# Feature tiles that stream both parts of the tokens behind one weight load

## The chip, the cores and the metric

One core of a Trainium2 chip runs the whole program. The metric is device time in microseconds, the median of a few runs on the chip. Beside the runs there is one profiled execution, with the start and length of every instruction.

## The reference

The reference computes two transformer blocks over 256 tokens of 1024 features, all in float32. The matrix products that matter here are projections of normed tokens `h`:

```
f  = (silu(h @ w_g) * (h @ w_u)) @ w_down            # twice, d_ff = 2816
q, k, v, z, xs, b, c, dt = split(h @ w_in)           # stick-breaking attention and a state-space mixer
xbc = silu(conv4(concat(xs, b, c)) + conv_b)         # depthwise, causal, 4 taps
q = h @ xa_wq ; k, v = split(mem_n @ xa_wkv)         # cross attention on a memory of 256 rows
c_gate, hc, b_gate, q, f_pre, v, g = split(h @ w_in_2)
u = c_gate * hc ; y = b_gate * conv3(u)              # and a gated recurrence that takes sigmoid(f_pre)
q = (h @ wq) ; scores = q . keys ; top 16 pairs      # 16384 experts: gelu(h . u_e) * gate, times v_e
```

Between the stages stand root-mean-square norms and residual sums. The answer must keep float32 accuracy.

## The kernel before

**Precision.** TensorE multiplies operands of a rounded float32 type. So the kernel splits each operand into a rounded part (hi) and what is left (lo), and forms hi x hi, hi x lo and lo x hi. The tokens' two parts are `uT[0]` and `uT[1]`, features on partitions: 8 tiles of 128 features by 256 tokens each. A weight *unit* is 128 x 1024 numbers, loaded by a DMA into `raw`, and split by `prefetch` (L127): ScalarE writes hi (L142), VectorE the rest lo (L143). A ring of slots holds split units some tiles ahead of their use.

**Kinds of product.** `half_chunk` and `acc_step` take tokens as the stationary operand and 512 columns of a unit as the moving one. A *feature tile* (`f_tile`, L297) is the other way round: 128 columns of the weight are stationary, and 256 tokens move through. It runs over 8 feature tiles k and makes three matmuls in each, all into the first half of one PSUM bank: w_hi x u_hi, w_hi x u_lo, w_lo x u_hi. Every matmul has its own weight load. Two banks `mm` alternate, so a tile needs the bank that the second-last tile left. After the 24 matmuls the function `evac` that the caller gave takes the result out of PSUM: one instruction on ScalarE or VectorE that also scales, adds a bias, or applies Silu, Sigmoid or a product.

**Where feature tiles stand.** In order of time: 36 in the first feed-forward stage (`features`, L499, a gate and an up tile by turns), 16 `qk` (L830), 1 `dt` (L836), 8 `xs` and 4 `bc` (L857, each with a 4-tap convolution in `conv`, L844), 8 `mk` (L906, from the memory's `memT`), 8 `xq` (L996), 36 in the second feed-forward stage, 4 `f2` (L1182, Sigmoid), 4 `q2` (L1187), 12 `chb` (L1202 to L1206, triples that end in a 3-tap convolution, L1191), 12 `pq` (L1433), and 128 `pu`, the experts' first table (L1477).

**What sets the order.** The program is written out by hand: each engine runs its instructions strictly in the order in which the Python code makes them. `tick` is called in the middle and at the end of a tile; after a given amount of products it takes the next step of each *side* (a generator with work of another kind, such as `attention`, `steps`, `hgrn`, `short_conv`), and at the end of a tile also the next split. So in the queue of VectorE and of ScalarE the order is: what the middle of the tile added, `evac` of the tile, the sides' steps at its end, the split.

**Side work that matters here.** `attention` (L570) walks through L585 (products), L596 and L597 (exponential, logarithm), L599 and L600 (sums on VectorE), L602 and L603 (split), L607 (products of the running sums), L611, L620. `steps` works on `dt`; L653 to L661 are its copies on VectorE. `hgrn` begins with a table load (L1035), four products on VectorE (L1038) and a logarithm (L1040), then L1042 and four scans (L1044). `short_conv` begins with transposes of the convolved tile (L1147), which PE meets in its own order.

Of the kernel before, what the change touches and what calls it, by code (L numbers as in the profile page):

```python
# [100 lines left out]
class Builder:  # L101
# [25 lines left out]
    def prefetch(self, n=1):  # L127
        """The parts of the next n units: rounded, and what is left."""
# [38 lines left out]
    def extend(self, slots, raws):  # L167
        """More places for units, split and just loaded, in the free parts of the arenas."""
        self.retired = False
        self.live = len(self.slots) + slots  # L170
        for _ in range(slots):
            b = self.RA.alloc(2048)
            self.free.append(len(self.slots))
            self.extra[len(self.slots)] = b
            self.slots.append((b.ap[:, 0:1024], b.ap[:, 1024:2048]))
        for _ in range(raws):
            b = self.FA.alloc_top(1024)
            self.raw_free.append(len(self.raw))
# [19 lines left out]
    def tick(self, us, split=True):  # L198
        """After us of products were issued: the next split, and as much of the side work."""
# [22 lines left out]
    def add_side(self, gen, rate):  # L222
        """gen yields where other work may come between, after 1 / rate us of it or what it yields."""
# [13 lines left out]
    def settle(self):  # L237
        """All but the norms at the end of a stage."""
# [20 lines left out]
    def half_chunk(self, u0, t, aT, evac, hook=None):  # L259
        """512 columns: [tokens, 512] for token tile t, from four units."""  # L260
# [29 lines left out]
    def opening(self, u0, aT, evacs, before_t1):  # L290
        """Two chunks, the first token tile of both ahead of the second."""
# [4 lines left out]

    def f_tile(self, u, aT, evac):  # L297
        """128 columns: [columns, 256 tokens], from one unit."""
# [35 lines left out]
    def acc_gemm(self, u0, pairs, n, done=None, mid=None, tail=6, early=1, before_t1=None, have=None):  # L334
        """[tokens, 1024] += one unit for each (features tile, index in it, position) of pairs. have(k): the
        features that unit k takes are there, for the first token tile."""
# [38 lines left out]
    def transposes(self, src, t, dst, col=None, kt0=0, n=8, part=None):  # L375
        """Tokens of tile t by features -> features by tokens, in two parts, times the gain."""
# [28 lines left out]
    def halves_rstd(self, ss):  # L405
        """From the two halves of a mean of squares."""
# [11 lines left out]
    def resid(self, t, row, ss):  # L418
        """h += rmsnorm(acc) * row; the mean squares of the new h to ss."""
# [21 lines left out]
    def normed(self, t, ss, hn):  # L441
        """h of token tile t, divided by its root mean square."""
# [20 lines left out]
    def ffn(self, name, row_name, before_t1, done, mid):  # L463
        """h += rmsnorm(swiglu(rmsnorm(h))) / 2."""
# [34 lines left out]
        def features(c):  # L499
            act[c] = self.tpair(2)  # L500
            ac = abs_[c % 2].v(j=2, t=256)
            for j in range(2):
                u, sg = u0 + FFN_AT["gu", c] + 2 * j, sgs[j].ap
                self.f_tile(u, uT, lambda ps: nc.scalar.activation(sg, ps, AF.Silu))
                self.f_tile(u + 1, uT, lambda ps: nc.vector.tensor_mul(ac[:, j], ps, sg))
# [63 lines left out]
    def attention(self, par, qT, kT, vt, oat, ready):  # L569
        """Stick-breaking attention, two heads at a time, keys on partitions."""  # L570
# [58 lines left out]
    def steps(self, dtb, dtT):  # L629
        """dt and its running sums, tokens on partitions."""  # L630
# [23 lines left out]
        # the sums with heads on partitions, in three parts that add up  # L654
# [23 lines left out]
    def ssd(self, xp, zt, oT, ready):  # L678
        """xp: [channels, 12, 3+256] convolved; y for both chunks, gated, normed, transposed."""
# [20 lines left out]
        # states after the first chunk  # L700
# [109 lines left out]
    def mixer(self, before_t1, done, mid):  # L810
# [10 lines left out]
        mblocks, memT = self.tpair(8)  # L821
# [7 lines left out]
        for f in range(8):  # L829
            self.f_tile(FIRST["qk"] + 2 * f, uT,  # L830
                        lambda ps: nc.scalar.activation(qT[:, f], ps, AF.Copy, scale=0.125))
            self.f_tile(FIRST["qk"] + 2 * f + 1, uT, lambda ps: nc.scalar.activation(kT[:, f], ps, AF.Copy))
# [3 lines left out]
        self.f_tile(FIRST["dt"], uT, lambda ps: nc.scalar.activation(  # L836
            dtT, ps[0:16], AF.Identity, bias=self.cols[0:16, COL["dt_bias"]:COL["dt_bias"] + 1]))
# [6 lines left out]
        def conv(f, ps):  # L844
            nc.scalar.activation(xp[:, f, 3:259], ps, AF.Copy)
# [10 lines left out]
        for f in range(8):  # L856
            self.f_tile(FIRST["xs"] + f, uT, lambda ps: conv(f, ps))  # L857
        for f in range(4):
            self.f_tile(FIRST["bc"] + f, uT, lambda ps: conv(8 + f, ps))
# [45 lines left out]
        for f in range(8):  # L905
            self.f_tile(FIRST["mk"] + f, memT, lambda ps: nc.vector.tensor_copy(kmT[:, f], ps))  # L906
# [18 lines left out]
    def cross(self, before_t1, kv, done, mid):  # L925
# [69 lines left out]
        for f in range(8):  # L995
            self.f_tile(FIRST["xq"] + f, uT,  # L996
                        lambda ps: nc.scalar.activation(qT[:, f], ps, AF.Copy, scale=0.0625))
# [31 lines left out]
    def hgrn(self, qh, ff, vt, gt, mix, ready):  # L1029
# [16 lines left out]
        # decays  # L1046
# [17 lines left out]
        # tokens by keys for the updates of the state  # L1064
# [17 lines left out]
        # states  # L1082
# [59 lines left out]
    def short_conv(self, f, y, yt, mix):  # L1142
        """The 128 channels of tile f: norm of their two groups, and to the features of mix."""
# [25 lines left out]
    def second(self, before_t1, done, mid):  # L1169
# [11 lines left out]
        for f in range(4):  # L1181
            self.f_tile(FIRST["f2"] + f, uT, lambda ps: nc.scalar.activation(ff[:, f], ps, AF.Sigmoid))  # L1182
# [3 lines left out]
        for f in range(4):  # L1186
            self.f_tile(FIRST["q2"] + f, uT, lambda ps: nc.scalar.activation(qh[:, f], ps, AF.Copy))  # L1187
# [3 lines left out]
        def conv(f, ps):  # L1191
            up, b = ups[:, f % 2], bg[:, f % 2]
            nc.scalar.activation(b, ps, AF.Copy)
# [6 lines left out]
        for f in range(4):  # L1200
            up = ups[:, f % 2]
            self.f_tile(FIRST["chb"] + 3 * f, uT,  # L1202
                        lambda ps: nc.scalar.activation(up[:, 2:258], ps, AF.Copy))
            self.f_tile(FIRST["chb"] + 3 * f + 1, uT,
                        lambda ps: nc.vector.tensor_mul(up[:, 2:258], up[:, 2:258], ps))
            self.f_tile(FIRST["chb"] + 3 * f + 2, uT, lambda ps: conv(f, ps))  # L1206
# [14 lines left out]
    def top16(self, lists):  # L1221
        """Of each list (source, its length, values, indices, scratch): the 16 best, in order."""
# [28 lines left out]
    def pick_head(self, sc, h):  # L1251
        """The 16 best pairs of keys of a head, both token tiles. Ranks (a, b) with more than 16 pairs at or
        above them are left out: for a = 0 all b stay, for a < 8 those under 8, and then b = 0."""
# [27 lines left out]
    def routing(self, kT):  # L1281
        """Experts and gates of both token tiles."""
# [3 lines left out]
        # places in the list of pairs -> ranks  # L1286
# [47 lines left out]
    def gates(self, kT, X):  # L1334
        """Gates of four tokens at a time, spread over all experts."""
# [34 lines left out]
    def peer(self):  # L1370
# [58 lines left out]
        for c in range(1, 4):  # L1429
            if c > 1:  # L1430
                self.finish(chunks[c - 2])
            for f in range(4):
                self.f_tile(FIRST["pq"] + 4 * c + f, hT, lambda ps: nc.scalar.activation(  # L1433
                    qT[c % 2][:, :, f], ps.rearrange("p (t n) -> p t n", t=2), AF.Copy))
# [324 lines left out]
```

## Time and profile before

| | |
|---|---|
| median of 3 runs | 1671.27 us (1669.7 to 1671.59) |
| span of the profiled execution, its own time | 1669.3 us |
| TensorE busy | 1652.0 us (99%) |
| VectorE busy | 1152.8 us (69%) |
| ScalarE busy | 981.0 us (59%) |
| GpSimd busy | 272.2 us (16%) |

The span runs from the first to the last instruction of the execution that the profiler recorded; no other time of that execution is given. A matmul's end is modelled and overlaps the next one's start, so the distance between starts tells more of TensorE's pace than its busy share. The granted TensorE clock is at its full level in all 40 slices of the page.

### The profile page before, as it was taken

To read this page: it belongs to the slowest core of one execution; us is meant where nothing else is said; L and a number is where in the kernel's file an instruction comes from. 1 tells how busy PE (TensorE), PEld (TensorE's weight loads), DVE (VectorE), ACT (ScalarE), POOL (GpSimd) and SP (SyncE) were. 2 spreads that over 40 slices of the span, in tenths; PEclk is the share of its full clock that TensorE was granted. 3 is DMA by queue.
4 is the path that set the end of the run, shared out by engine and by line. 5 is a ranking of instruction groups with operands and counts; after the bars stand their busy time and mean duration, and the time that the engine had idled before them with its cause. 6 is when DMAs were issued, how large, how long until landed. Compare 5 with 4: busy or idle time off the path is not lost.

```text
span 1669.3 us, 29176 instructions
## 1 busy us (share of the span) xinstructions
PE 1652.0 (99%) x11110; PEld 1504.8 (90%) x11110; DVE 1152.8 (69%) x2369; ACT 981.0 (59%) x1826; POOL 272.2 (16%) x312
## 2 busy tenths in 40 slices
PE   8999999999999999999999999999999999999998
PEld 6999899988898899989989999999999888888886
DVE  7555565876756755567657998899999855555554
ACT  7444476786555644457355564888877645545544
POOL 0000000000000000000100002988888100000000
PEclk9999999999999999999999999999999999999999
DMA  9565443354535856536234555445444555555553
GB/s 333 196 199 184 159 133 125 112 197 147 176 101 170 272 183 199 186 102 201 77 128 154 180 183 190 153 165 165 160 158 154 192 198 189 194 197 190 194 196 127
DMA packets 79325, 288.77 MB, mean 173 GB/s; under 512 B 8784, under 2 KB 8912, under 8 KB 79056
## 3 DMA queue, kind: packets, MB, share of 16 engines
q1 hardware_dynamic: 77904, 281.66, 50.9%
q10 hardware_dynamic: 1280, 5.24, 0.9%
q8 instruction: 87, 1.43, 0.4%
q14 instruction: 54, 0.44, 0.1%
HBM read 285.82 MB, written 1.05 MB: 172 GB/s over the span
## 4 chain that ended last, share of the span: by engine, by line
PE 93%; DVE 2%; ACT 2%; DMA 1%; issue 1%; POOL 0%; SPq 0%; POOLq 0%; ACTq 0%; DVEq 0%
PE mm L305 15%; PE mm L306 15%; PE mm L307 15%; PE acc L322 11%; PE acc L324 11%; PE acc L326 11%; PE mm L276 2%; PE mm L272 2%; PE mm L273 2%; PE sd L1356 2%; DMA raw<-ws 1%; DVE lo L143 1%; PE sd L383 1%; PE acc L585 1%; PE sd L1411 0%
## 5 line engine op out<-in xcount | busy, mean ns | idle before, releaser
L143 DVE TENSOR_TENSOR lo<-raw,hi 128x1024 fp32r<-128x1024 f32 x419 | 513.3, 1228 | 266.0 <-ACT hi L142 263.9
L305 PE MATMUL mm<-uT,hi 128*128 128x256 f32 x2024 | 580.9, 287 | 1.9 <-DVE X L1459 1.0
L306 PE MATMUL mm<-uT,hi 128*128 128x256 f32 x2024 | 571.2, 282 | 0.0
L307 PE MATMUL mm<-uT,lo 128*128 128x256 f32 x2024 | 571.1, 282 | 0.0
L142 ACT ACTIVATE hi<-raw 128x1024 fp32r<-128x1024 f32 x419 | 442.1, 1058 | 218.7 <-PE acc L326 185.6
L305 PEld LDWEIGHTS mm<-uT,hi 128*128 128x128 f32 x2024 | 385.9, 191 | 4.4 <-DVE X L1459 1.7
L306 PEld LDWEIGHTS mm<-uT,hi 128*128 128x128 f32 x2024 | 386.1, 191 | 0.8
L307 PEld LDWEIGHTS mm<-uT,lo 128*128 128x128 f32 x2024 | 385.9, 191 | 0.0
L1343 POOL TENSOR_SCALAR m<-iota,kT 128x128 f16<-128x128 f16 x256 | 233.9, 931 | 204.0 <-DVE kT L1326 154.2
L322 PE MATMUL acc<-hi,uT 128*128 128x512 f32 x536 | 166.1, 391 | 0.0
L326 PE MATMUL acc<-hi,uT 128*128 128x512 f32 x536 | 165.5, 389 | 0.0
L324 PE MATMUL acc<-lo,uT 128*128 128x512 f32 x536 | 165.4, 389 | 0.0
L411 POOL TENSOR_TENSOR hr<-hv,mhalf 128x1 f32<-128x1 f32 x26 | 15.2, 587 | 817.4 <-DVE hv L410 817.4
L143 DVE TENSOR_TENSOR lo<-fa,hi 128x1024 fp32r<-128x1024 f32 x74 | 90.1, 1224 | 65.6 <-ACT hi L142 65.2
L326 PEld LDWEIGHTS acc<-hi,uT 128*128 128x128 f32 x536 | 100.6, 188 | 21.1
L324 PEld LDWEIGHTS acc<-lo,uT 128*128 128x128 f32 x536 | 100.6, 188 | 21.0
L322 PEld LDWEIGHTS acc<-hi,uT 128*128 128x128 f32 x536 | 100.4, 188 | 21.2 <-issue 0.5
L1456 ACT ACTIVATE X<-mm 128x256 f32<-128x256 f32 (+40 forms) x126 | 39.8, 316 | 107.3 <-PE mm L307 106.4
L142 ACT ACTIVATE hi<-fa 128x1024 fp32r<-128x1024 f32 x74 | 77.4, 1056 | 43.2 <-PE mm L306 24.3
L1345 ACT ACTIVATE oh<-m,kT 128x128 f16<-128x128 f16 x256 | 81.1, 390 | 0.0
L322 PE MATMUL acc<-hi,ra 128*128 128x512 f32 x216 | 70.9, 410 | 0.6 <-ACT ra L1164 0.6
L324 PE MATMUL acc<-lo,ra 128*128 128x512 f32 x216 | 67.3, 393 | 0.0
(358 smaller groups left out, 2364.2 us busy)
## 6 DMA issues: line engine op xcount, KB each, us to landing
raw<-ws SPq DMA_DIRECT2D x443, 512.0 KB, 3.3
fa<-ws SPq DMA_DIRECT2D x90, 512.0 KB, 3.4
fa<-rows ACTq DMA_DIRECT2D x5, 512.0 KB, 4.3
fa<-mem ACTq DMA_DIRECT2D x1, 1024.0 KB, 7.0
X<-keysT ACTq DMA_DIRECT2D x1, 1024.0 KB, 4.7
out<-X SPq DMA_DIRECT2D x4, 256.0 KB, 2.0
h<-x SPq DMA_DIRECT2D x2, 256.0 KB, 2.8
h<-x SPq DMA_DIRECT2D x1, 512.0 KB, 7.2
```

The source lines that it names most:

```text
L142: nc.scalar.activation(hi, raw, AF.Copy)
L143: nc.vector.tensor_sub(lo, raw, hi.bitcast(F32))
L272: nc.tensor.matmul(ps, ah[:, k, ts], wh, start=(k == 0), stop=False)
L305: nc.tensor.matmul(ps, wh, ah[:, k, :], start=(k == 0), stop=False)
L306: nc.tensor.matmul(ps, wh, al[:, k, :], start=False, stop=False)
L307: nc.tensor.matmul(ps, wl, ah[:, k, :], start=False, stop=(k == 7))
L322: nc.tensor.matmul(o[h], ah[:, k, ts], hi[:, hs[h]], start=first, stop=False)
L324: nc.tensor.matmul(o[h], ah[:, k, ts], lo[:, hs[h]], start=False, stop=False)
L326: nc.tensor.matmul(o[h], al[:, k, ts], hi[:, hs[h]], start=False, stop=last)
L1343: nc.gpsimd.tensor_scalar(m1[:, i], self.iota, key(0, i), None, op0=OP.is_equal)
L1345: nc.scalar.activation(oh[:, i], m1[:, i], AF.Copy, scale=key(2, i))
L1456: nc.scalar.activation(X[:, i, g:256], ps[:, g:256], AF.Gelu)
```

## The change

Feature tiles, all but the 128 `pu` tiles, become *wide tiles*. The tokens' two parts now lie in one tile, `uB`, so that one matmul can stream u_hi and u_lo (512 rows) past w_hi. It fills both halves of a bank: the first with w_hi x u_hi, the second with w_hi x u_lo. The third product, w_lo x u_hi (256 rows), adds to the second half. In place of 24 matmuls of 256 rows a tile has 8 of 512 and 8 of 256. On the way out the halves are added: `sum` copies the second half to the output on ScalarE, and VectorE adds the first half to it. What was fused into the one instruction before follows as another: Silu, Sigmoid, the product with the gate. The memory's two parts get one block (`memB`) in place of two. Docstrings and comments also fall away.

```diff
+    def sum(self, out, ps, scale=None, bias=None):
+        nc, (a, b) = self.nc, ps
+        if bias is not None:
+            nc.scalar.activation(out, b, AF.Identity, bias=bias)
+        else:
+            nc.scalar.activation(out, b, AF.Copy, scale=scale or 1.0)
+        if scale:
+            nc.vector.scalar_tensor_tensor(out, a, scale, out, op0=OP.mult, op1=OP.add)
+        else:
+            nc.vector.tensor_add(out, a, out)
+
+    def wide_tile(self, u, both, evac):
+        nc = self.nc
+        ps = self.mm().rearrange("p (s t) -> p s t", s=2)
+        hi, lo = self.get(u)
+        for k in range(8):
+            wh, wl = hi[:, k * 128:k * 128 + 128], lo[:, k * 128:k * 128 + 128]
+            if k < 7:
+                nc.tensor.matmul(ps, wh, both[:, :, k, :], start=(k == 0), stop=False)
+            nc.tensor.matmul(ps[:, 1], wl, both[:, 0, k, :], start=False, stop=False)
+            if k == 7:
+                nc.tensor.matmul(ps, wh, both[:, :, k, :], start=False, stop=True)
+            if k == 3:
+                self.tick(1.3, False)
+        self.release(u)
+        evac((ps[:, 0], ps[:, 1]))
+        self.tick(1.3)
...
-                self.f_tile(u, uT, lambda ps: nc.scalar.activation(sg, ps, AF.Silu))
-                self.f_tile(u + 1, uT, lambda ps: nc.vector.tensor_mul(ac[:, j], ps, sg))
+                def gate(ps):
+                    self.sum(sg, ps)
+                    nc.scalar.activation(sg, sg, AF.Silu)
+
+                def up(ps):
+                    self.sum(ac[:, j], ps)
+                    nc.vector.tensor_mul(ac[:, j], ac[:, j], sg)
+                self.wide_tile(u, self.uB, gate)
+                self.wide_tile(u + 1, self.uB, up)
...
         def conv(f, ps):
-            nc.scalar.activation(xp[:, f, 3:259], ps, AF.Copy)
+            self.sum(xp[:, f, 3:259], ps)
...
-            self.f_tile(FIRST["f2"] + f, uT, lambda ps: nc.scalar.activation(ff[:, f], ps, AF.Sigmoid))
+            def evf(ps):
+                self.sum(ff[:, f], ps)
+                nc.scalar.activation(ff[:, f], ff[:, f], AF.Sigmoid)
+            self.wide_tile(FIRST["f2"] + f, self.uB, evf)
...
         def conv(f, ps):
             up, b = ups[:, f % 2], bg[:, f % 2]
-            nc.scalar.activation(b, ps, AF.Copy)
+            self.sum(b, ps)
             nc.vector.tensor_scalar(y[:, f], up[:, 0:256], cw[:, 0, f:f + 1], None, op0=OP.mult)
...
-            self.uT = tuple(st.tile([128, 8, 256], F32R, name=f"uT{i}") for i in range(2))
+            self.uB = st.tile([128, 2, 8, 256], F32R, name="uT")
+            self.uT = tuple(self.uB[:, i] for i in range(2))
```

The tiles `qk`, `dt`, `mk`, `xq`, `q2`, the other `chb` and `pq` change alike: `wide_tile` with `sum` as the way out. The calls of `tick`, and so the order of side work and splits, stay as they were.

## Rows read from the trace of the kernel before

**Rows 1.** The page: busy time of each engine, and the last chain by engine.
```profile
PE 1652.0 (99%) x11110; PEld 1504.8 (90%) x11110; DVE 1152.8 (69%) x2369; ACT 981.0 (59%) x1826; POOL 272.2 (16%) x312
...
PE 93%; DVE 2%; ACT 2%; DMA 1%; issue 1%; POOL 0%; SPq 0%; POOLq 0%; ACTq 0%; DVEq 0%
```

**Rows 2.** Windows, the `bc` tiles: length, then busy us of PE, PEld, DVE, ACT, POOL.
```profile
328.40:341.30 12.90, 12.90 (x112) 12.90 (x110) 12.54 (x25) 8.92 (x16) 0.00 (x0) 1.00 0.56 182
```

**Rows 3.** Timeline of PE, first feed-forward stage: start us, us, what, count.
```profile
103.85 0.63 PE L322 MATMUL acc<-hi,ra 128*128 128x512 f32 x2
...
108.85 0.62 PE L326 MATMUL acc<-hi,ra 128*128 128x512 f32 x2
109.31 0.28 PE L305 MATMUL mm<-uT,hi 128*128 128x256 f32 x1
...
111.91 0.28 PE L306 MATMUL mm<-uT,hi 128*128 128x256 f32 x1
```

**Rows 4.** Timeline of PE where one matmul of 512 and two of 256 follow.
```profile
319.38 0.39 PE L607 MATMUL acc<-ra,ntri 128*128 128x512 f32 x1
...
319.85 0.40 PE L607 MATMUL acc<-ra,ntri 128*128 128x512 f32 x1
```

**Rows 5.** Lines, first feed-forward stage: busy us, mean ns, idle before and releaser.
```profile
L143 DVE TENSOR_TENSOR lo<-fa,hi 128x1024 fp32r<-128x1024 f32 x24 | 29.4, 1225 | 29.5 <-ACT hi L142 29.5
L142 ACT ACTIVATE hi<-fa 128x1024 fp32r<-128x1024 f32 x24 | 25.4, 1058 | 20.6 <-PE mm L306 12.2 <-PE acc L326 8.4
L505 DVE TENSOR_TENSOR fa<-mm,fa 128x256 f32<-128x256 f32 x18 | 7.6, 425 | 3.8 <-PE mm L307 3.8
```

**Rows 6.** Timeline of ACT, DVE and PE around the fifth to eighth `xs` tile.
```profile
317.64 0.39 ACT L845 ACTIVATE fa<-mm 128x256 f32<-128x256 f32 x1
318.06 0.51 ACT L848 ACTIVATE fa<-fa,cols 128x256 f32<-128x256 f32 x1
...
326.20 1.00 DVE L850 SCALAR_TENSOR_TENSOR fa<-fa,cols 128x256 f32<-128x256 f32 x2
...
324.10 0.28 PE L305 MATMUL mm<-uT,hi 128*128 128x256 f32 x1
```

**Rows 7.** Timeline of DVE, the last `bc` tiles.
```profile
339.85 1.00 DVE L850 SCALAR_TENSOR_TENSOR fa<-fa,cols 128x256 f32<-128x256 f32 x2
...
342.41 0.48 DVE L850 SCALAR_TENSOR_TENSOR fa<-fa,cols 128x256 f32<-128x256 f32 x1
```

**Rows 8.** Timeline of ACT: first and fourth `f2` tile, first `q2` tile.
```profile
756.80 0.38 ACT L1182 ACTIVATE fa<-mm 128x256 f32<-128x256 f32 x1
...
763.23 0.39 ACT L1182 ACTIVATE fa<-mm 128x256 f32<-128x256 f32 x1 [1.16 <-PE mm L307]
...
768.31 0.36 ACT L1187 ACTIVATE fa<-mm 128x256 f32<-128x256 f32 x1
```

**Rows 9.** Timeline of PE: starts of the third and fourth `q2` tile.
```profile
768.78 0.33 PE L305 MATMUL mm<-uT,ra 128*128 128x256 f32 x1
...
771.67 0.28 PE L305 MATMUL mm<-uT,ra 128*128 128x256 f32 x1
```

**Rows 10.** Timeline of DVE in `q2`.
```profile
767.34 0.69 DVE L1042 TENSOR_SCALAR fa<-fa 128x1024 f32<-128x1024 f32 x1
768.43 2.44 DVE L1044 TENSOR_TENSOR_SCAN fa<-seg,fa 128x256 f32<-128x256 f32 x4 [0.40 <-ACT fa L1040]
```

**Rows 11.** Timeline of DVE, ACT and PE after the first `chb` triple.
```profile
782.60 0.35 DVE L1194 TENSOR_SCALAR fa<-fa,cols 128x256 f32<-128x256 f32 x1
782.98 1.01 DVE L1196 SCALAR_TENSOR_TENSOR fa<-fa,cols 128x256 f32<-128x256 f32 x2
784.10 0.42 DVE L1198 TENSOR_TENSOR fa<-fa 128x256 f32<-128x256 f32 x1
...
783.26 0.38 ACT L1193 ACTIVATE fa<-mm 128x256 f32<-128x256 f32 x1 [1.92 <-PE mm L307]
...
784.58 0.44 PE L1147 MATMUL sd<-ident,fa 128*128 128x128 f32 x2
```

More of the change, by code (lines that the diff above doesn't have):

```diff
@@ L820, in mixer @@
         self.opening(FIRST["v"], uT, [evv(0), evv(1)], before_t1)
-        mblocks, memT = self.tpair(8)
+        memb2 = self.RA.alloc(4096)
+        memB = memb2.v(s=2, k=8, t=256)
+        mblocks, memT = (memb2,), (memB[:, 0], memB[:, 1])
         qb, kb, ob = (F.alloc(2048) for _ in range(3))
@@ L829, in mixer, with evq @@
         for f in range(8):
-            self.f_tile(FIRST["qk"] + 2 * f, uT,
-                        lambda ps: nc.scalar.activation(qT[:, f], ps, AF.Copy, scale=0.125))
-            self.f_tile(FIRST["qk"] + 2 * f + 1, uT, lambda ps: nc.scalar.activation(kT[:, f], ps, AF.Copy))
+            def evq(ps):
+                self.sum(qT[:, f], ps, 0.125)
+            self.wide_tile(FIRST["qk"] + 2 * f, self.uB, evq)
+            self.wide_tile(FIRST["qk"] + 2 * f + 1, self.uB, lambda ps: self.sum(kT[:, f], ps))
             ready[0] = (f + 1) // 2
@@ L835, in mixer @@
         dtT = dtb.ap[0:16]
-        self.f_tile(FIRST["dt"], uT, lambda ps: nc.scalar.activation(
-            dtT, ps[0:16], AF.Identity, bias=self.cols[0:16, COL["dt_bias"]:COL["dt_bias"] + 1]))
+        self.wide_tile(FIRST["dt"], self.uB, lambda ps: self.sum(
+            dtT, [p[0:16] for p in ps], bias=self.cols[0:16, COL["dt_bias"]:COL["dt_bias"] + 1]))
         self.add_side(self.steps(dtb, dtT), 2.25)
@@ L856, in mixer @@
         for f in range(8):
-            self.f_tile(FIRST["xs"] + f, uT, lambda ps: conv(f, ps))
+            self.wide_tile(FIRST["xs"] + f, self.uB, lambda ps: conv(f, ps))
         for f in range(4):
-            self.f_tile(FIRST["bc"] + f, uT, lambda ps: conv(8 + f, ps))
+            self.wide_tile(FIRST["bc"] + f, self.uB, lambda ps: conv(8 + f, ps))
         self.drain()
@@ L905, in mixer @@
         for f in range(8):
-            self.f_tile(FIRST["mk"] + f, memT, lambda ps: nc.vector.tensor_copy(kmT[:, f], ps))
+            self.wide_tile(FIRST["mk"] + f, memB, lambda ps: self.sum(kmT[:, f], ps))
         assert ready[1]
@@ L995, in cross, with evq @@
         for f in range(8):
-            self.f_tile(FIRST["xq"] + f, uT,
-                        lambda ps: nc.scalar.activation(qT[:, f], ps, AF.Copy, scale=0.0625))
+            def evq(ps):
+                self.sum(qT[:, f], ps, 0.0625)
+            self.wide_tile(FIRST["xq"] + f, self.uB, evq)
             ready[0] = (f + 1) // 2
@@ L1186, in second @@
         for f in range(4):
-            self.f_tile(FIRST["q2"] + f, uT, lambda ps: nc.scalar.activation(qh[:, f], ps, AF.Copy))
+            self.wide_tile(FIRST["q2"] + f, self.uB, lambda ps: self.sum(qh[:, f], ps))
         ready[0] = 1
@@ L1201, in second, with evh @@
             up = ups[:, f % 2]
[L1202 to L1206, printed above, removed]
+            def evh(ps):
+                self.sum(y[:, f], ps)
+                nc.vector.tensor_mul(up[:, 2:258], up[:, 2:258], y[:, f])
+            self.wide_tile(FIRST["chb"] + 3 * f, self.uB, lambda ps: self.sum(up[:, 2:258], ps))
+            self.wide_tile(FIRST["chb"] + 3 * f + 1, self.uB, evh)
+            self.wide_tile(FIRST["chb"] + 3 * f + 2, self.uB, lambda ps: conv(f, ps))
             gen = self.short_conv(f, y[:, f], yt[:, f % 2], mix)
@@ L1432, in peer @@
             for f in range(4):
-                self.f_tile(FIRST["pq"] + 4 * c + f, hT, lambda ps: nc.scalar.activation(
-                    qT[c % 2][:, :, f], ps.rearrange("p (t n) -> p t n", t=2), AF.Copy))
+                self.wide_tile(FIRST["pq"] + 4 * c + f, self.uB, lambda ps: self.sum(
+                    qT[c % 2][:, :, f], [p.rearrange("p (t n) -> p t n", t=2) for p in ps]))
             scores(c)
```

## The prediction

> **What bounds the kernel now.** I read the chain that ended last first: the reader is to see that TensorE makes 93% of it and no other engine over 2% [rows 1]. So a matmul saved is time saved, until another engine is late for it. Then, stretch by stretch, how busy the others are: over the four `bc` tiles VectorE works 12.54 of 12.90 us [rows 2]. There its queue runs behind without harm, since ScalarE alone empties the PSUM bank.
>
> **The change part by part.** It touches 149 tiles: 72 in the two feed-forward stages, 16 `qk`, 1 `dt`, 8 `xs`, 4 `bc`, 8 `mk`, 8 `xq`, 4 `f2`, 4 `q2`, 12 `chb`, 12 `pq`. My times are those of the profiled execution; its span of 1669.3 us lies 2.0 below the median of the runs, and I add the 2.0 at the end.
>
> *The matmuls.* 24 of 256 rows become 8 of 512 and 8 of 256: as many rows, 8 weight loads fewer. In a feature tile 22 matmuls start over 111.91 - 109.31 = 2.60 us, 118.2 ns each; 22 of 512 rows start over 108.85 - 103.85 = 5.00 us, 227.3 ns each [rows 3]. So a wide one saves 2 x 118.2 - 227.3 = 9.1 ns over two narrow ones, a tile 73 ns (2.77 us for 2.84), 149 tiles 10.9 us. Two bounds. Where both shapes alternate, 512 + 256 + 256 rows start over 319.85 - 319.38 = 0.47 us [rows 4]; less two narrow ones at 118 ns, the wide one costs 234 ns there: 2 to 3 ns saved, 3 us in all. Upwards, 256 more rows cost 227.3 - 118.2 = 109.1 ns; a wide one of 218 ns would save 147 ns a tile, 22 us. The two stretches in the moving operand have no row; I keep 9.1 ns, from the form and stage nearest to it. A rule speaks against this: the Trainium skill ("TensorE: Matmul & The Clock Gate", "Back-to-back issue gap") gives an isolated gap of N/2.4 + 2.5 ns, 109.2 and 215.8 ns, so the pair would save 2.6 ns and all tiles 3 us (an estimate from the page). The trace disagrees with it at 256 rows (118.2 ns) and at 512 (227.3 ns) [rows 3].
>
> *The way out.* One instruction (a copy on ScalarE) becomes a copy of one half and, waiting for it, an add on VectorE; the nearest row is VectorE's product out of PSUM, 0.42 us [rows 5]. Sigmoid, Silu and the product with it become further instructions. What counts is the wait: the bank is free only after VectorE's add, and the second-next tile takes that bank. Queued ahead of the add is everything VectorE was given before; queued behind it is the next split, and ScalarE waits for the add wherever it reads the sum. A handover from engine to engine I take as 0.05 us, an estimate that no row shows by itself.
>
> *Feed-forward stages.* A gate and an up tile together need on VectorE: add 0.42, the wait for Silu (0.38, as the copies of [rows 8]) and the next rounding (1.06) on ScalarE, the split's rest 1.22, add 0.42, product 0.42, rest 1.22 [rows 5]: 5.14 us at most, against 5.54 us of PE. They hide; without that cover the pair would pay the difference. 72 x 73 ns = -5.3 us.
>
> *`qk`, `dt`, `mk`, `xq`.* The reader of a `qk`, `mk` or `xq` tile comes a tile or more later, and VectorE has room. 33 x 73 ns = 2.4; I give back 0.6 for attention's steps that stand behind an add: -1.8 us (ends -2.4 and +1).
>
> *`xs` and `bc`.* Each convolution now runs copy, add, ScalarE's first product (L848), VectorE's three, and the split in between. In the trace L848 of the fifth `xs` tile starts at 318.06, and from it a chain with no gap (attention's exponentials on ScalarE, its sums on VectorE, the copies of the `dt` side work, the split's rest) leads to VectorE's first product for the sixth tile at 326.20 [rows 6]: 8.14 us. The sixth tile's add must stand ahead of that product; the eighth tile needs its bank and began at 324.10 [rows 6]. Even with nothing late before, the fifth add cannot end before 317.64 + 0.39 + 0.05 + 0.42 = 318.5 (copy, handover, add), so the eighth tile begins at 318.5 + 0.05 + 8.14 + 0.42 = 327.1: +3.0 us. The fifth add itself is late by earlier waits of this kind, 0 to 3 us; I take 2. In the last tiles VectorE's products and split repeat every 342.41 - 339.85 = 2.56 us [rows 7]; add 0.42, L848's 0.51 and two handovers of 0.05 make 3.6, against 2.77 on PE: 0.8 for each of the last three banks, +2.4 (the two before them have attention's matmuls as cover). Together +7.4 us, the 12 tiles' own gain not counted (ends +2.5, the bare lateness of the row, and +10).
>
> *`f2` and `q2`.* The first `f2` copy stands behind a table load and begins at 756.80, long after its tile; before, ScalarE catches up and is prompt at the fourth, 763.23 [rows 8]. Now add, Sigmoid, rounding, rest, add is one loop over both queues: 0.42 + 0.05 + 0.29 + 1.06 + 0.03 + 1.14 = 2.99 us (add, handover, Sigmoid, rounding, handover, rest, with the lengths of [rows 5, 8]; neighbours on one queue overlap by some 0.1, an estimate, and without that the loop is 3.2), slower than a tile of 2.77, so nothing is caught up. The first add begins at 757.23, the fourth ends at 757.23 + 3 x 2.99 + 0.42 = 766.6: the fourth Sigmoid is 3.4 us late. From it to the first `q2` copy, through a table load and a logarithm, ScalarE needs 768.31 - 763.23 = 5.08 us [rows 8], then comes the add: that bank is free at 772.5, where the third `q2` tile began at 768.78 [rows 9]: +3.7. VectorE then has a product of 0.6 and four scans of 2.44 [rows 10] and a rest of 1.14 ahead of the second `q2` add (0.42): 777.1 for the fourth tile, which began at 771.67 [rows 9]: +5.3 us, the tiles' gain included (ends +1 and +6.5).
>
> *`chb`.* The sum of the third tile of each triple now heads the convolution, whose products L1194 to L1198 (0.35 + 1.01 + 0.42) began before the copy (782.60 against 783.26). Now: 783.26 + 0.38 + 0.05 + 0.42 + 0.05 + 1.78 = 785.95 where PE transposes the result at 784.58 [rows 11]: PE stands 1.4 us, and as long at the last triple; the middle two have state updates as cover, 0.3 each. +3.4, less 12 x 73 ns: +2.5 us (ends 0 and +4).
>
> *`pq`.* Gain 0.9; scores that follow a tile at once wait for an add, twice 0.42 as estimate: 0.
>
> Sum: -5.3 - 1.8 + 7.4 + 5.3 + 2.5 = +8.1. 1669.3 + 8.1 + 2.0 = **1679.4 us**: slower. What is late next is VectorE's add ahead of a feature tile.
>
> **The rivals.** (a) *Faster: lateness isn't carried on.* The queues catch up after each wait, and only the bare ones remain: 3.0 at the eighth `xs` tile, 0.9 at `q2` (add and handovers), 2.8 in `chb`; against 10.9 gained, -4.2: 1667. For it: VectorE is busy only 69% over all [rows 1]. Against it: the 8.14 us chain has no gap. It decides at the fourth `f2` Sigmoid: within 1 us of its tile, this rival holds. (b) *Slower still: the wide matmul is worth nothing*, as the mixed row has it (a form of this: each half still gets its own load and the change doesn't do what it says). The 129 tiles counted above as PE-bound then gain 22 ns for 73: 6.5 us more, 1686. By the formula of the Trainium skill ("TensorE: Matmul & The Clock Gate", "Back-to-back issue gap") the time would be the same 1686, an estimate from the page. (c) *No change*: waits at half my price (about 9 of 18 us) cancel the gain: 1671.
>
> **How the numbers follow.** My forecast 0.50 (own range 1674.7 to 1685), (b) 0.20, (a) 0.15, (c) 0.15. About 0.2% (3.3 us) is what can be told from no change: faster 0.15 (a), same 0.15 (c), slower 0.70. The range goes from 1666 (just beyond a) to 1688 (b, with the upper end of one wait).
>
> **What would show it.** 1192 weight loads fewer; feed-forward stages 2.6 us shorter each; starts of wide ones 227 ns apart from their narrow neighbour; PE waiting for VectorE's adds at the seventh and eighth `xs` tile, the last two `bc` tiles and the first product of `z`, the third and fourth `q2` tile, and L1147's transposes behind the convolution. I am wrong if the stretch from `xs` to `bc` is no longer than before, or if the third `q2` tile starts less than 1 us late against the first `f2` tile.

## The result, and the profile after

The changed kernel takes 1688.4 us (median of 4 runs, 1687.2 to 1688.5), the kernel before 1671.35 beside it: 1.0104 of its time, 95% interval 1.0092 to 1.0116, so 17.0 us slower. The direction was forecast and the size was not: 9.0 us above the forecast, 0.4 us above the end of the range. The profiled execution has a span of 1686.7 us, 17.4 more than the one before.

The page of the kernel after: busy time of each engine, and the last chain by engine.
```profile
PE 1656.0 (98%) x9918; PEld 1448.3 (86%) x9918; DVE 1203.8 (71%) x2510; ACT 1011.7 (60%) x1914; POOL 270.4 (16%) x312
...
PE 89%; DVE 5%; ACT 3%; issue 2%; DMA 1%; POOL 0%; SPq 0%; POOLq 0%; ACTq 0%; DVEq 0%
```
Against [rows 1]: 1192 matmuls and weight loads fewer, just what 149 tiles x 8 make, 141 instructions more on VectorE, and in the chain VectorE has gone from 2% to 5%. The waits of TensorE say for what (columns: engine, tile and line that waited, what it waited for; us in total, times, longest):
```profile
PE mm L318 <- DVE fa L307: 7.3, 5, 2.7
...
PE sd L1189 <- DVE fa L1243: 2.6, 2, 1.3
PE sd L1457 <- DVE X L307: 2.3, 2, 1.2
PE acc L645 <- ACT ra L640: 1.3, 2, 1.1
```
L318 is the wide matmul, L307 VectorE's add of the halves, L1189 the transposes of the short convolution (L1147 before), L1457 the scores of the experts' search. (A wait of 6.8 us for L477, left out here, stands in the kernel before too, with 6.6 us.)

Where the time went, by when TensorE reaches the same tile in the two traces (us gained or lost within a stage):

| stage | forecast | measured |
|---|---|---|
| both feed-forward stages | -5.3 | -1.62 - 1.44 = -3.1 |
| `qk`, `dt`, `mk`, `xq` | -1.8 | -0.46 - 0.04 - 0.42 - 0.44 = -1.4 |
| `xs`, `bc` | +7.4 | +10.3 |
| `f2`, `q2` | +5.3 | +0.5 + 5.8 = +6.3 |
| `chb` | +2.5 | +1.4 + 1.6 = +3.0 |
| `pq` | 0 | +1.9 |
| sum | +8.1 | +17.0 |

The rest of the 17.4 us lies outside these stages. Every stage that was to gain gains and every one that was to lose loses; each came out worse than forecast. The three places:

*The wide matmul.* Timeline of TensorE in the first feed-forward stage (start us, us, line and operation, count):
```profile
109.04 0.39 PE L318 MATMUL mm<-uT,hi 128*128 128x512 f32 x1
109.27 0.28 PE L319 MATMUL mm<-uT,lo 128*128 128x256 f32 x1
...
111.47 0.40 PE L318 MATMUL mm<-uT,hi 128*128 128x512 f32 x1
...
114.28 0.39 PE L318 MATMUL mm<-uT,hi 128*128 128x512 f32 x1
```
The last two of these lines begin tiles, so a tile takes 114.28 - 111.47 = 2.81 us. After a wide matmul the next starts 0.23 us later; over the 1043 such pairs of the trace the median is 233 ns, and 117 ns after a narrow one.

*The eighth `xs` tile.* VectorE, ScalarE and TensorE after the seventh:
```profile
325.00 0.36 ACT L303 ACTIVATE fa<-mm 128x256 f32<-128x256 f32 x1
...
327.02 1.23 DVE L143 TENSOR_TENSOR lo<-raw,hi 128x1024 fp32r<-128x1024 f32 x1
328.16 0.42 DVE L307 TENSOR_TENSOR fa<-mm,fa 128x256 f32<-128x256 f32 x1
328.61 0.51 ACT L889 ACTIVATE fa<-fa,cols 128x256 f32<-128x256 f32 x1 [3.25 <-DVE fa L307]
328.63 0.79 PE L318 MATMUL mm<-uT,hi 128*128 128x512 f32 x1 [2.71 <-DVE fa L307]
...
336.48 0.63 PE L318 MATMUL mm<-uT,hi 128*128 128x512 f32 x1
```
The copy (L303) is done at 325.36; the add waits until 328.16 behind the work of the `dt` side job and a split (L143), and TensorE stands 2.71 us. The tile starts 4.5 us later than before [rows 6], though TensorE had come to `xs` 2.1 us early. And it then lasts 7.9 us, its side work included, where 4.2 passed before: the windows (length; busy us of PE, PEld, DVE, ACT, POOL; granted clock of TensorE; DMA share, GB/s) show a clock that fell to 0.50, 1.2 of 2.4 GHz, after a stretch in which TensorE had worked 2.10 of 5.00 us.
```profile
325.00:330.00 5.00, 2.10 (x7) 1.66 (x8) 4.22 (x11) 1.75 (x6) 0.00 (x0) 0.71 0.14 40
330.00:335.00 5.00, 5.00 (x22) 4.61 (x21) 3.96 (x8) 3.31 (x6) 0.00 (x0) 0.50 0.48 171
775.00:780.00 5.00, 2.30 (x9) 1.80 (x8) 3.61 (x10) 3.65 (x6) 0.00 (x0) 0.76 0.32 105
780.00:785.00 5.00, 5.00 (x18) 4.24 (x18) 5.00 (x9) 3.19 (x4) 0.00 (x0) 0.55 0.31 102
```
The kernel before has 1.00 in all of these. No term of the prediction held such a fall. (The second fall is not in every execution: see the kernel with fillers below.)

*`f2` and `q2`.* The Sigmoids of the last three `f2` tiles, the add of the first `q2` tile, and the starts of the third and fourth:
```profile
766.50 0.42 ACT L1226 ACTIVATE fa<-fa 128x256 f32<-128x256 f32 x1 [1.36 <-DVE fa L307]
769.49 0.42 ACT L1226 ACTIVATE fa<-fa 128x256 f32<-128x256 f32 x1 [1.36 <-DVE fa L307]
772.49 0.42 ACT L1226 ACTIVATE fa<-fa 128x256 f32<-128x256 f32 x1 [1.36 <-DVE fa L307]
...
777.81 0.42 DVE L307 TENSOR_TENSOR fa<-mm,fa 128x256 f32<-128x256 f32 x1 [1.39 <-ACT fa L303]
778.29 0.79 PE L318 MATMUL mm<-uT,ra 128*128 128x512 f32 x1 [2.70 <-DVE fa L307]
783.58 0.63 PE L318 MATMUL mm<-uT,ra 128*128 128x512 f32 x1
```
The Sigmoids come 2.99 us apart, the loop of the prediction to the last digit.

### The profile page after: what moved, and what is told of

It reads as the page before. It is cut to its first block, busy times and chain, and to the rows that moved or that the text cites. A ratio compares the mean times of both kernels' runs of the same rounds, so it can differ in the third digit from the quotient of the medians.

```text
span 1686.7 us, 26981 instructions
## 1 busy us (share of the span) xinstructions
PE 1656.0 (98%) x9918; PEld 1448.3 (86%) x9918; DVE 1203.8 (71%) x2510; ACT 1011.7 (60%) x1914; POOL 270.4 (16%) x312
## 3 DMA queue, kind: packets, MB, share of 16 engines
HBM read 285.82 MB, written 1.05 MB: 170 GB/s over the span
## 4 chain that ended last, share of the span: by engine, by line
PE 89%; DVE 5%; ACT 3%; issue 2%; DMA 1%; POOL 0%; SPq 0%; POOLq 0%; ACTq 0%; DVEq 0%
PE mm L318 12%; PE acc L353 11%; PE acc L355 11%; PE acc L357 11%; PE mm L319 7%; PE mm L336 7%; PE mm L338 7%; PE mm L337 7%; PE mm L276 2%; PE mm L273 2%; PE mm L272 2%; PE mm L321 2%; DVE lo L143 2%; PE sd L1402 2%; DMA raw<-ws 1%
## 5 line engine op out<-in xcount | busy, mean ns | idle before, releaser
L143 DVE TENSOR_TENSOR lo<-raw,hi 128x1024 fp32r<-128x1024 f32 x419 | 513.0, 1228 | 241.1 <-ACT hi L142 239.6
L318 PE MATMUL mm<-uT,hi 128*128 128x512 f32 x875 | 320.8, 403 | 4.9 <-DVE fa L307 4.6
L336 PE MATMUL mm<-uT,hi 128*128 128x256 f32 x1024 | 295.0, 288 | 1.0 <-DVE X L1505 1.0
L337 PE MATMUL mm<-uT,hi 128*128 128x256 f32 x1024 | 289.3, 283 | 0.0
L338 PE MATMUL mm<-uT,lo 128*128 128x256 f32 x1024 | 289.2, 282 | 0.0
L319 PE MATMUL mm<-uT,lo 128*128 128x256 f32 x1000 | 261.1, 282 | 0.0
L318 PEld LDWEIGHTS mm<-uT,hi 128*128 128x128 f32 x875 | 165.6, 189 | 41.0 <-DVE fa L307 6.2
L336 PEld LDWEIGHTS mm<-uT,hi 128*128 128x128 f32 x1024 | 195.9, 191 | 1.8 <-DVE X L1505 1.7
L337 PEld LDWEIGHTS mm<-uT,hi 128*128 128x128 f32 x1024 | 196.0, 191 | 0.0
L303 ACT ACTIVATE fa<-mm 128x256 f32<-128x256 f32 x136 | 52.0, 382 | 116.6 <-PE mm L321 116.4
L143 DVE TENSOR_TENSOR lo<-fa,hi 128x1024 fp32r<-128x1024 f32 x74 | 90.0, 1222 | 40.1 <-ACT hi L142 39.6
```

What stands on the lines that cost most here:

```text
L143: nc.vector.tensor_sub(lo, raw, hi.bitcast(F32))
L303: nc.scalar.activation(out, b, AF.Copy, scale=scale or 1.0)
L318: nc.tensor.matmul(ps, wh, both[:, :, k, :], start=(k == 0), stop=False)
L319: nc.tensor.matmul(ps[:, 1], wl, both[:, 0, k, :], start=False, stop=False)
L336: nc.tensor.matmul(ps, wh, ah[:, k, :], start=(k == 0), stop=False)
L337: nc.tensor.matmul(ps, wh, al[:, k, :], start=False, stop=False)
```

## The experiments

Times are medians; the kernel before, run beside each, took 1670.6 to 1671.4, and differences go against that run. My theory by then was the table above: the way out costs where VectorE's queue is late, each stage by itself, and the half clock makes some 5 us of it.

**Narrow again, stage by stage.** Four kernels put the tiles of some stages back as they were, in this manner:
```diff
-            self.wide_tile(FIRST["q2"] + f, self.uB, lambda ps: self.sum(qh[:, f], ps))
+            self.f_tile(FIRST["q2"] + f, uT, lambda ps: nc.scalar.activation(qh[:, f], ps, AF.Copy))
```


> Only the 72 tiles of the two ff stages are wide, the other 77 are as before. If a wide tile is worth what its lag shows in the kernel after (ff1 1.62 us and ff2 1.44 us earlier, 43 ns a tile): 1671.3 - 3.1 = 1668.2. If it is worth the 73 ns of the prediction: 1671.3 - 5.3 = 1666.0. If a wide matmul is worth nothing (233 ns beside 2 x 117 ns): 1671.3. Both losses, at the xs and bc stages and at f2 and q2, should be gone, and with them the two falls of the granted clock.

> The kernel after, with the 12 tiles of xs and bc as before. If the loss there is made by their own way out (the adds behind VectorE's queue), all 10.3 us of lag that the two stages added go: 1688.4 - 10.3 = 1678.1, and the clock does not fall near 327 us. If the loss comes from the lateness of VectorE that the qk tiles before them bring on, or is given back later by waits that it hides now, less comes back: over 1681.

> The kernel after, with the 8 tiles of f2 and q2 as before. If their own way out is the loss: 1688.4 - 6.3 = 1682.1, and the clock does not fall near 778 us. If the second mixer's chain (its scans on VectorE) sets the end of the stage anyway, nothing comes back: 1688.4.

> Wide only where the lag fell in the kernel after: both ff stages, qk, dt, mk and xq (105 tiles); xs, bc, f2, q2, chb and pq as before. If the stages are independent: 1671.3 - 1.62 - 1.44 - 0.46 - 0.04 - 0.42 - 0.44 = 1666.9. If a wide tile is worth 73 ns: 1663.6. If the adds of the qk tiles make xs late too, part of the loss stays: 1668 to 1671.

| kernel | us | against before | expected |
|---|---|---|---|
| only feed-forward wide | 1667.8 | -3.1 (0.9983, 0.9974 to 0.9992) | 1668.2 |
| `xs`, `bc` narrow | 1677.5 | +6.6 | 1678.1 |
| `f2`, `q2` narrow | 1682.2 | +11.4 | 1682.1 |
| wide only where it gains | 1667.9 | -2.9 (0.9983, 0.9974 to 0.9992) | 1666.9 |

Each loss belongs in the main to the stage's own tiles: 17.05 - 6.64 = 10.4 us for `xs` and `bc`, 17.05 - 11.36 = 5.7 for `f2` and `q2`. The stages are independent only to about 1 us: where the `qk` tiles are wide and the `xs` tiles narrow (second and last kernel), `xs` still loses 0.9 us in the traces, at attention's products of the running sums (L645, L607 before); in the first kernel, with `qk` narrow, it loses nothing. A wide tile without a wait is worth 3.1 / 72 = 43 ns. The first and the last kernel are faster than the kernel before, by 0.17%. They are alike within their intervals, so the 1.4 us that `qk`, `dt`, `mk` and `xq` show in the trace is not established by the times; the 0.9 us at `xs` takes more than half of it back.

One expectation of the first kernel failed in its trace: `q2` loses 3.6 us there with narrow tiles, behind a wait of 1.8 us for ScalarE's copy, and the granted clock is 0.80 from 765 to 770 us. That execution took 1671.4 us, the ten others 1666.6 to 1669.1. So a late `q2` can come without an add; what made it late there was not followed up.

**No add at all.** The two lines of the add are gone from the helper that empties a bank; one half of each product is then missing from the output.
```diff
-        if scale:
-            nc.vector.scalar_tensor_tensor(out, a, scale, out, op0=OP.mult, op1=OP.add)
-        else:
-            nc.vector.tensor_add(out, a, out)
```


> The kernel after without the add on VectorE: each bank is left to ScalarE's copy of one half alone, so the other half is missing from the output. All 149 tiles stay wide. If the adds behind VectorE's queue are the whole loss, what is left is the gain of the stream, 149 x 43 ns = 6.4 us, and no stretch at half clock: 1671.0 - 6.4 = 1664.6. If a wide stream itself loses in those stages (by weight loads or the clock), it stays above 1675.

1665.5 us, 5.3 below before, all 149 tiles wide. The loss comes with the adds: without them no stage of the trace loses more than 0.4 us (`q2`), and the granted clock is 1.00 in the windows of the two falls. Whether it is the adds' length or their place in the queue, this kernel can't tell.

**The old matmuls with the new way out.** The opposite cut: 24 narrow matmuls, into the two halves of a bank.
```diff
-                nc.tensor.matmul(ps, wh, both[:, :, k, :], start=(k == 0), stop=False)
+            nc.tensor.matmul(ps[:, 0], wh, both[:, 0, k, :], start=(k == 0), stop=False)
+            nc.tensor.matmul(ps[:, 1], wh, both[:, 1, k, :], start=False, stop=False)
```


> All 149 tiles by 24 matmuls of 256 rows each, as before, but into the two halves of a bank with the copy and the add of the kernel after. If the way out makes the loss: the time of after and the gain of the stream lost besides, 1688.4 + 6.4 = 1694.8 (1692 to 1695, since a stalled tile hides its gain). If the wide matmuls make it: about 1671.

1692.2 us, 21.4 above before: the price of the way out alone. With the one before it: of the 5.3 us that the stream can give, the kernel after keeps 21.36 - 17.05 = 4.3.

**TensorE kept busy through the waits**, to take the half clock away and leave the waits.
```diff
+    def fill(self, u, n):
+        ps = self.sd()
+        hi = self.get(u)[0]
+        for i in range(n):
+            k = i % 4 * 2
+            nc = self.nc
+            nc.tensor.matmul(ps, hi[:, k * 128:k * 128 + 128], self.uT[0][:, k:k + 2, :], start=True, stop=True)
...
+            if f == 7:
+                self.fill(FIRST["xs"] + f, 11)
```


> The kernel after with 5 and 11 matmuls of 512 rows into an unused bank of PSUM at the two idle stretches of TensorE ahead of the eighth xs tile, and 11 ahead of the third q2 tile, about 2.6 us where TensorE waited 2.7 us. If the half clock after the waits costs what the tiles show (3.6 us at xs, 1.3 us at q2): the clock stays at full speed and the time is 1688.4 - 4.9 = 1683.5. If VectorE sets the pace of these tiles whatever the clock, or the clock falls for another reason: 1688.4, or up to 1690 by the fillers themselves.

1687.6 us, 0.2 less against before than the change itself (its interval is 14.0 to 19.5 above before; my 4.9 us would leave about 12). The clock did stay up, as the windows of this kernel show (columns as above):
```profile
325.00:330.00 5.00, 4.61 (x22) 3.39 (x21) 4.24 (x10) 1.75 (x5) 0.00 (x0) 1.00 0.10 16
330.00:335.00 5.00, 5.00 (x36) 4.60 (x35) 3.98 (x7) 3.65 (x8) 0.00 (x0) 1.00 0.54 181
```
So my 5 us for the clock are refuted; a worth of up to 3 us is not excluded by the times. Where the gain went at `xs` and `bc` is in its timeline, the adds of the last `bc` tiles and the matmuls that wait for them:
```profile
340.56 0.41 DVE L307 TENSOR_TENSOR fa<-mm,fa 128x256 f32<-128x256 f32 x1
341.02 0.50 PE L318 MATMUL mm<-uT,hi 128*128 128x512 f32 x1 [0.71 <-DVE fa L307]
344.13 0.41 DVE L307 TENSOR_TENSOR fa<-mm,fa 128x256 f32<-128x256 f32 x1
344.60 0.50 PE L318 MATMUL mm<-uT,hi 128*128 128x512 f32 x1 [0.49 <-DVE fa L307]
347.69 0.42 DVE L307 TENSOR_TENSOR fa<-mm,fa 128x256 f32<-128x256 f32 x1
348.17 0.50 PE L272 MATMUL mm<-hi,uT 128*128 128x512 f32 x1 [0.37 <-DVE fa L307]
```
Here TensorE, at full clock, waits for three more adds, 3.56 and 3.57 us apart: the three banks and the 3.6 us of the prediction. In the kernel after it computes so slowly in between that these waits have nothing left to show. `z` starts at 348.17 for 349.58; one wait more, of 1.3 us for the state work's VectorE (L742), takes the rest. Half clock and late adds cover each other here, and VectorE sets the end of the stage either way.

At `q2` it is otherwise. Four more kernels (`xs` and `bc` narrow, and three that follow below) have the same wait of 2.7 us at the third `q2` tile, and their clock stayed at 1.00, as in the first of those that follow:
```profile
775.00:780.00 5.00, 2.27 (x13) 1.76 (x12) 3.60 (x8) 3.72 (x6) 0.00 (x0) 1.00 0.43 148
```
There the third tile lasts 4.4 us where it lasts 783.58 - 778.29 = 5.3 in the kernel after, and `q2` loses 4.6 us for 5.8. So in that trace the half clock cost about 1 us at `q2`, and such a wait brings it in some executions only.

**Why a wide matmul takes 233 ns.** Two tries: the two parts side by side in SBUF, and another order of the 16 matmuls.
```diff
-            self.uB = st.tile([128, 2, 8, 256], F32R, name="uT")
+            self.uB = st.tile([128, 8, 2, 256], F32R, name="uT")
```


> The kernel after with the two parts of a feature block next to each other in SBUF, so that a wide matmul reads 512 neighbouring columns, where it now reads two pieces of 256 that lie 2048 columns apart. If the two pieces are why a wide matmul takes 233 ns and not the 227 ns of the other 512-row matmuls, 6 ns x 8 in some 129 tiles without a wait come back: 1688.4 - 6.2 = 1682.2. If the 6 ns belong to the change between 512 and 256 rows: 1688.4.

> The kernel after with another order of the 16 matmuls of a wide tile: one of 512 rows, then the eight of 256, then seven of 512, where it now alternates. If the alternation makes a wide matmul 233.7 ns long where others of 512 rows take 227 to 231: 3 to 6 ns x 8 in some 129 tiles without a wait, 1688.4 - (3 to 6) = 1682 to 1685. If any 512-row matmul with a weight load of its own takes as long: 1688.4.

1687.0 and 1686.1 us; the intervals (1.0078 to 1.0112 and 1.0077 to 1.0111) hold the ratio of the change itself, and both spans, 1686.6 and 1686.5, equal its 1686.7. A tile of the second in the trace:
```profile
108.94 0.40 PE L318 MATMUL mm<-uT,hi 128*128 128x512 f32 x1
109.18 1.10 PE L319 MATMUL mm<-uT,lo 128*128 128x256 f32 x8
110.12 1.80 PE L322 MATMUL mm<-uT,hi 128*128 128x512 f32 x7
111.76 0.40 PE L318 MATMUL mm<-uT,hi 128*128 128x512 f32 x1
```
(1.10 - 0.28) / 7 = 117 ns and (1.80 - 0.40) / 6 = 233 ns again, 2.82 us a tile. Neither the two pieces nor the alternation makes it. Nor is it peculiar to the wide tile: the kernel before has it in `half_chunk`, where only matmuls of 512 rows follow each other, four starts in 0.93 us:
```profile
31.09 0.39 PE L272 MATMUL mm<-hi,uT 128*128 128x512 f32 x1
...
32.02 0.62 PE L276 MATMUL mm<-hi,uT 128*128 128x512 f32 x2
```
What makes it 233 ns here and 227 there stays open.

**`chb` and `pq`.** The products of the short convolution go ahead of the copy and the add, and the `pq` tiles are narrow again (not shown).
```diff
         def conv(f, ps):
             up, b = ups[:, f % 2], bg[:, f % 2]
-            self.sum(b, ps)
             nc.vector.tensor_scalar(y[:, f], up[:, 0:256], cw[:, 0, f:f + 1], None, op0=OP.mult)
...
+            self.sum(b, ps)
             nc.vector.tensor_mul(y[:, f], y[:, f], b)
```


> The kernel after with two edits in separate stages. In chb the three products of the short convolution are issued ahead of the copy and the add of the third tile, so that only the add and one multiplication are left when its bank is full; the 12 pq tiles are as before. If the transposes of chb wait for that chain and the scores of pq for the adds: 2.6 us less at chb (the wait of the transposes goes) and 1.9 us less between pq and the next stage, 1688.4 - 4.5 = 1683.9. If the short convolution waits for the second mixer's work on VectorE anyway, only pq's part comes back: 1686.5; if pq's lag comes from the search of the experts, only chb's: 1685.8.

1684.2 us, 3.4 less against before than the change; in the traces TensorE loses 1.7 us less over `chb`, where its waits for L1243 shrink from 2.6 to 0.9 us, and 1.9 less over `pq`. Both causes hold. Two differences of this execution lie elsewhere and cancel: `q2` lost 1.2 us less, with its clock at 1.00, and the stretch from `bc` to `mk` 1.3 more.

**Whose adds, and in which order.** Left open was whether the 16 us of `xs`, `bc`, `f2` and `q2` come from the adds' load on VectorE or from how the queues hang on each other. First GpSimd adds the halves, which ScalarE has copied to SBUF whole, so no bank waits for VectorE.
```diff
+        self.nc.scalar.activation(x, self.mmb[self.mm_i % 2], AF.Copy)
+        self.nc.gpsimd.tensor_tensor(out, x[:, 0:256], x[:, 256:512], op=OP.add)
```


> Wide in all stages but pq; in xs, bc, f2, q2 and chb ScalarE copies the whole bank of 512 columns to SBUF, which frees it, and GpSimd adds the halves there: no bank waits for VectorE. If the loss of these stages is the bank's wait for VectorE's queue, it goes and the gain of the stream is left: 1671.0 - 4.4 (ff, qk, dt, mk, xq as their lags show) - 32 x 0.045 = 1665.2 (1665 to 1667). If the wait only moves to ScalarE, which stands still for GpSimd's sum ahead of the first tap and of the sigmoid: 1670 to 1680. If every two-step way out costs as much, whichever engine does it: over 1683.

1686.2 us, where `pq` alone should have given 1.9 back: nothing is regained at the other stages together. My number and the second one are refuted; the time lies where the third reading put it (over 1683), that every way out in two steps costs as much. By stages the total hides a shift: `xs` loses 5.2 us for 10.3, but from `mk` to `xq` 3.2 us are lost where 0.3 were gained, and TensorE's transposes wait 2.0 us for VectorE there, and `f2` and `q2` lose 0.9 more. Its timeline over two `f2` tiles:
```profile
764.05 1.23 DVE L143 TENSOR_TENSOR lo<-raw,hi 128x1024 fp32r<-128x1024 f32 x1 [2.89 <-ACT hi L142]
764.58 1.29 POOL L313 TENSOR_TENSOR fa<-fa 128x256 f32<-128x256 f32 x1 [1.96 <-ACT fa L312]
765.91 0.42 ACT L1236 ACTIVATE fa<-fa 128x256 f32<-128x256 f32 x1 [1.40 <-POOL fa L313]
766.23 1.04 ACT L142 ACTIVATE hi<-raw 128x1024 fp32r<-128x1024 f32 x1
767.18 0.58 ACT L312 ACTIVATE fa<-mm 128x512 f32<-128x512 f32 x1
767.31 1.23 DVE L143 TENSOR_TENSOR lo<-raw,hi 128x1024 fp32r<-128x1024 f32 x1 [2.03 <-ACT hi L142]
767.84 1.30 POOL L313 TENSOR_TENSOR fa<-fa 128x256 f32<-128x256 f32 x1 [1.96 <-ACT fa L312]
```
A bank is now emptied by ScalarE, but ScalarE still stands 1.40 us for the sum ahead of each Sigmoid, with the next rounding and the next copy queued behind: the loop is 767.84 - 764.58 = 3.26 us, longer than 2.99. So the loop was never VectorE's alone. The next two kernels open it: the taps of `xs` and `bc` and the Sigmoid are issued one tile later, with the adds on VectorE, then on GpSimd (`chb` and `pq` narrow in both).
```diff
+        held = []
+
         def conv(f, ps):
             self.sum(xp[:, f, 3:259], ps)
+            held.append(f)
+            while len(held) > (f < 11):
+                taps(held.pop(0))
```


> The kernel after with chb and pq as before (worth 4.9 us by their lags: 1683.5), and the first tap of xs and bc and the sigmoid of f2 issued one tile later, behind the next tile's copy and add, so that neither ScalarE nor VectorE stands still for the other inside a tile's way out. If the loss at xs, bc, f2 and q2 is this crossing from ScalarE to VectorE and back in two queues that keep their order: most of 16 us goes, what stays is VectorE's 3.1 us a tile in bc (add 0.42, three taps 1.46, one split 1.22) beside 2.82 and the adds among the scans of the second mixer: 1670 to 1674. If it is the adds' load on VectorE: 1680 to 1683.5.

> The same, with the halves of xs, bc, f2 and q2 copied whole by ScalarE and added by GpSimd. VectorE then has the load of before. If the crossing is the loss, 1667.9 (only ff, qk, dt, mk and xq wide) less 20 x 0.045: 1667.0 (1666 to 1669). If a bank is freed too late whenever a second engine is on the way out: over 1675.

1675.6 us (4.2 above before) and 1674.7 (3.3 above). Against 12.1 above before, which the kernel with both `chb` and `pq` undone would have by the table (17.0 - 4.9, an estimate; that kernel was not run), the later taps bring 7.9 us back with every add still on VectorE: about half of the 16 us was the crossing, not the load. The traces say the same by stages: `xs` and `bc` lose 5.1 us for 10.4, `f2` and `q2` 3.1 for 6.3. Both rivals were half right; the first kernel lies between their numbers, and the second is 5.7 us over the range that I gave it and just under the rival's 1675.

In the trace of the second `xs` and `bc` lose only 1.4 us and `f2` and `q2` 1.6, but 4.0 us are lost from `mk` to `xq`, where TensorE's transposes wait 2.9 us for VectorE (L429), and 1.1 at `chb` with its narrow tiles. So its time is not the price of its adds alone. That TensorE comes earlier to work that is no earlier is my reading of these waits; no run shows it apart. What is left in the first, VectorE ahead of the eighth `xs` tile:
```profile
324.07 0.28 DVE L697 CAST part<-fa 16x256 bf16<-16x256 f32 x1
324.50 1.23 DVE L143 TENSOR_TENSOR lo<-raw,hi 128x1024 fp32r<-128x1024 f32 x1
324.71 0.39 ACT L303 ACTIVATE fa<-mm 128x256 f32<-128x256 f32 x1
325.65 0.42 DVE L307 TENSOR_TENSOR fa<-mm,fa 128x256 f32<-128x256 f32 x1
326.12 0.79 PE L318 MATMUL mm<-uT,hi 128*128 128x512 f32 x1 [2.32 <-DVE fa L307]
```
The add now stands only behind other work in VectorE's queue (side job and split), and still TensorE waits 2.32 us. An add in front of a bank's release is late there by whatever VectorE was given before it.

## Why the prediction was right or wrong

The mechanism and the direction were right. What failed are terms of the sum: the gain of a wide matmul (73 ns a tile, measured 43), the price of the waits at `xs` and `bc` (+7.4 us, measured +10.3, the largest miss), `pq` (nothing, measured +1.9), and a fall of the clock that no term held.

- **What bounds the kernel, and the direction**: right. A matmul saved is time saved until VectorE is late; without the add all 149 tiles gain (1665.5), with it the lateness costs 21.4 us.
- **The matmuls**: the size failed. Of its two bounds I kept 9.1 ns a pair, from the 227.3 ns of [rows 3], and passed over the mixed row [rows 4], which gave 234 ns for a 512-row matmul among 256-row ones. The runs show 233 ns: 43 ns a tile for 73, 2.2 us less over the feed-forward stages. Those 227.3 ns belong to one stage and one form, matmuls that accumulate weights as the moving operand; other matmuls of 512 rows in the trace of before already took 231 to 234 ns, so one row was too little to choose by. That the mixed row had the right number was not because of the mixture, as the experiments show. Rival (b) had this length, though not the saving (22 ns a tile). Of the Trainium skill's formula ("TensorE: Matmul & The Clock Gate", "Back-to-back issue gap"), which gives 109.2 and 215.8 ns, the trace again agrees with neither (117 and 233 ns), though the small saving that follows from it was nearer than mine.
- **Feed-forward, `qk`, `mk`, `xq`, the way out**: right, hidden. TensorE waits for no add there. The handover of 0.05 us fits the rows: the add ends at 328.58, ScalarE starts at 328.61 and TensorE at 328.63.
- **`xs` and `bc`**: mechanism right, price too low by 3 us. The eighth tile came 4.5 us late where 5.0 was forecast, but I had counted from the times of before, and TensorE arrived 2.1 us early: against its own arrival the loss was 6.6. A tile that comes earlier gains nothing if what it waits for does not come earlier too. Of `bc`'s +2.4 the loop was right (3.57 us where 3.6 was forecast, in the kernel with fillers); in the kernel after the half clock stood in its place with 3.8.
- **`f2` and `q2`**: right. Loop 2.99 as forecast; taking off the 5.9 us by which the stage began late, the fourth Sigmoid is 772.49 - 5.9 - 763.23 = 3.4 us late (forecast 3.4), the third `q2` tile 3.6 (3.7), the fourth 6.0 (5.3). That excess is the half clock: where the clock stayed up (five other traces with wide `f2` and `q2` tiles) the fourth is 5.2 to 5.4 us late. The point at which rival (a) was to decide went clearly against it.
- **`chb`**: right; two waits of 1.3 us where 1.4 was forecast.
- **`pq`**: the step that failed by its kind. "Scores that follow a tile at once wait for an add, twice 0.42" priced the add and not the queue: in this stage VectorE searches the 16 best keys of each head, the add stands behind that, and the scores waited 1.1 and 1.2 us. Narrow `pq` tiles gave 1.9 us back.
- **The range**: its upper end was made of rival (b) and the upper end of one wait. But the terms that failed share one mechanism, an add behind VectorE's queue (at `f2` and `q2` with the half clock behind it), so they erred together, by +2.9, +1.0, +0.5 and +1.9, and what the matmuls and their cover fell short (2.2 + 0.4) came on top. Their upper ends should have been added. Rival (c) was mis-added too: waits of 9 us against a gain of 10.9 leave 1669.4, not 1671; nothing hung on it.

## What to carry to other kernels

Before work that empties a PSUM bank is moved to a second engine, price the bank's release by the queue of that engine at that place, not by the length of the new instruction: here 0.42 us of add cost up to 2.7 us of wait. When a tile's way out goes from one engine to another and back (copy, add, Sigmoid), the two queues lock into a loop whose period is the sum of what stands in both (here 2.99 and 3.57 us, against 2.81 for a tile); issue the step that comes back one tile later, which here returned about half of the loss of those stages. And take the change only for the stages whose neighbours have room: with 105 of the 149 tiles, or the 72 of the feed-forward stages alone, it is 0.17% faster than the kernel before, while all of them make it 1.0% slower.

## What the runs showed of the hardware

- In the trace of the kernel after, TensorE's granted clock fell to 0.50 after each of the two long waits, and was back at 1.00 some ten us later at `xs` and some seven at `q2`. At `xs` holding it up gave nothing in the end, since the engine that had made TensorE wait was still the later one; at `q2` other traces with the same wait kept 1.00 and lost 1.2 us less in the stage. A stretch at half clock behind a wait is a mark of the wait, and only in part a cost of its own.
- GpSimd's addition of 128x256, in the kernel that first uses it, took 0.74 us alone and up to 1.79 us beside a split of VectorE (L143 at 344.83 for 1.22 us), 721 ns at least over the 32 of them. The Trainium skill ("GPSIMD Engine Reference", "1. Specifications") says that GpSimd shares its way to SBUF with VectorE and contends with instructions of two SBUF inputs, as the split is; the trace agrees. VectorE pays as well: in the last kernel a tap of `bc` took 1.05 us beside an addition and 0.48 alone, 0.57 more, where the add that left VectorE had taken 0.42. This is a part of why the adds on GpSimd did not bring what they took from VectorE. (The first line is of the first kernel with GpSimd, the others are of the last.)
```profile
344.86 1.79 POOL L313 TENSOR_TENSOR fa<-fa 128x256 f32<-128x256 f32 x1 [2.05 <-ACT fa L312]
...
339.66 1.05 DVE L908 SCALAR_TENSOR_TENSOR fa<-fa,cols 128x256 f32<-128x256 f32 x1
339.69 0.74 POOL L313 TENSOR_TENSOR fa<-fa 128x256 f32<-128x256 f32 x1 [2.91 <-ACT fa L312]
...
348.09 0.48 DVE L908 SCALAR_TENSOR_TENSOR fa<-fa,cols 128x256 f32<-128x256 f32 x1
```
- Matmuls of 512 rows are not of one length. From start to start the median is 227 ns for those into `acc` in the first feed-forward stage and in the last stage, 227 to 232 in the stages between, 227 to 234 by place in `half_chunk`, and 233 in the wide tiles. What makes the difference was not found.
